# Two more operand pairs for the context's weight columns, a group of adaLN rows on TensorE, and x's squares moved up, in a one-core hybrid diffusion layer

## The chip, the cores and the metric

The kernel runs on 1 core of one Trainium2 chip. The metric is the device time of one execution in microseconds, the median of 3 runs. TensorE (PE in the profile) multiplies, VectorE (DVE) and ScalarE (ACT) work on tiles in SBUF and PSUM, GpSimd (POOL) on tiles in SBUF, and SyncE (SP) issues most of the DMAs.

## The reference, cut to what matters

One layer (DEPTH = 1) of a trunk over 2048 latent tokens of width 1024, with a context of 256 tokens in front. What the changed code computes is the beginning:

```python
ada   = silu(c) @ w_ada + b_ada            # (1, 6*1024), for the latent
ada_c = silu(c_ctx) @ w_ada + b_ada        # (6*1024,), for the context
sh1, sc1, g1, sh2, sc2, g2 = split(ada, 6);  csh1, csc1, ... = split(ada_c, 6)
hc = rmsnorm(ctx, norm_mix) * (1 + csc1) + csh1
logf_f, k_f, logf_b, k_b, vc = hgrn2_gates(hc @ w_in[:, :3 * 512])   # context: gates and values only
h  = rmsnorm(x, norm_mix) * (1 + sc1) + sh1
o  = token_mixers(h @ w_in, start states of the context)             # two gated scans, a gMLP
```

Behind that come the output projection, a gated MLP with a 3x3 convolution, and a final norm. All is float32, and a product that counts is made of three: each operand is split into a high part (rounded to TensorE's fp32r) and a low part (the rest), and hi·hi, hi·lo and lo·hi are summed in PSUM.

## The kernel before, in words

The edited code is the first 100 us. There is a part under `tc.manual_schedule()`, in which every engine takes its instructions in the order in which they are written; what follows is ordered by the framework's scheduler, with `pin` keeping single instructions in place, and with two task queues (`hg_q`, `bg_q`) whose steps are due by a count of TensorE work (`T.t`).

**adaLN.** The first 2048 columns of `w_ada` (shift and scale) are loaded as four groups of 512 columns: groups 0 and 1 (the shift) into the tile of tag `xl`, groups 2 and 3 (the scale) into that of tag `xh`. Later `xl` and `xh` hold x's low and high parts. `ada_products(g, k0, k1)` multiplies a group on TensorE with both vectors (context and latent) at once: eight products with a 128x512 block each, into a `pj` bank; `ada_rows` copies the two rows on ACT, `ada_columns` turns them into columns with four small transposes, `put_ada` adds the bias. Groups 0, 2 and 3 go that way. Group 1 goes by `ada_sums(w, k0, k1)`: for `w` = 1 (context) and `w` = 0 (latent), DVE adds eight scaled blocks into `acc` (L290), and `ada_ones` sums over partitions with four small products with `ones`.

**Context columns.** Each of the 12 context blocks (`keys` (column, CTX)) takes 128 columns of `w_in`: for head 0 the columns at 0, HW and 2·HW (first, second and third column below), for head 1 three more, and so on. `load_raw` loads a column to one of three `raw` tiles, `split_w` splits it: ACT casts the high part `whi` (L131), DVE or POOL subtracts for the low part `wlo` (L132; `w_n` counts the splits and picks the engine). There are two pairs of `whi`/`wlo` tiles, numbered in `w_free`; a pair is free again when the block's last product is done. A context block is 24 products of 128x256 (8 values of k, three each); its gate sigmoids (L547, L548, into `cS` for head 0 and `cf` for head 1) or its copy to `vv` follow on ACT. `ctx_mod(k)` makes the context's operands `ch`/`cl`. The first block's products for k = 0 to 3 are opened by hand (`opened`), and `run_banks` does the rest.

**x.** `x_start` takes x's first four rows of tiles (`xg`): ACT squares them (L232), POOL makes the root, DVE scales all four (L238), TensorE transposes them, and `x_mod` modulates (L243, `xfl`) and splits into `xh`/`xl`. Then the same with the next four (`xk`). Meanwhile `ctx_state` runs the context's scan on DVE in levels (L501 on `cS` or `cf`, L508 on `tot`). `misc` loads the masks and casts them on DVE (L461).

Of the kernel before, what the change touches and what calls it, by code (L numbers as in the profile page):

```python
# [10 lines left out]
F32R = mybir.dt.float32r  # L11
# [7 lines left out]
P = 128  # L19
D = 1024  # L20
NK = D // P
SEQ = 2048
TH = SEQ // 2
# [60 lines left out]
def tile_trunk(ctx, tc, x, c, cx, c_ctx, w_ada, b_ada, norm_mix, norm_ffn, w_in, hg_norm, sgu_g, sgu_b,  # L84
# [44 lines left out]
    def split(hi, lo, raw, eng=None, keep=lambda i: i):  # L129

        keep(S.copy(hi, raw))  # L131
        (eng or G).tensor_sub(lo, raw, hi.bitcast(F32))  # L132

    def mm3(ps, lhi, llo, rhi, rlo, first, last):
        T.matmul(ps, lhi, rhi, start=first, stop=False)
        T.matmul(ps, lhi, rlo, start=False, stop=False)
        T.matmul(ps, llo, rhi, start=False, stop=last)


    class Pump:  # L140
# [3 lines left out]
        def __init__(self):  # L144
            self.tasks, self.soon, self.at = [], [], 0.0
# [43 lines left out]
    with es1:  # L189
# [16 lines left out]
        def raw_tile():  # L206
            return p1.tile([P, D], F32, tag="raw", name="raw", bufs=3)

        w_n, w_raw, w_free = [0], {}, [0, 1]

        def load_raw(key):
            raw = raw_tile().rearrange("p (k c) -> p k c", c=P)
# [3 lines left out]
        def split_w(key, eng=None):  # L216
            if key not in w_raw:
                load_raw(key)
            raw, at = w_raw.pop(key), w_free.pop(0)
            hi = p1.tile([P, NK, P], F32R, tag=f"whi{at}", name="whi", align_bytes=AL)  # L220
            lo = p1.tile([P, NK, P], F32R, tag=f"wlo{at}", name="wlo", align_bytes=AL)
            w_n[0] += 1
            split(hi, lo, raw, eng or (V if w_n[0] < 8 or w_n[0] < 20 and w_n[0] % 2 else G))
            return hi, lo, at

        def x_sums():
            return pm.tile([P, 8], F32, tag="xss", name="xss", bufs=2)
# [50 lines left out]
        def ada_rows(g, tag):  # L278
            rows[g] = pm.tile([2, 512], F32, tag=tag, name="rows", bufs=2)
            S.copy(rows[g], pa.pop(g)[:2, :])  # L280
# [7 lines left out]
        def ada_sums(w, k0, k1):  # L288
            for k in range(k0, k1):
                V.scalar_tensor_tensor(out=acc[:, w, :], in0=wts[1, k // 4][:, k % 4, :], scalar=cs2[:, k, w:w + 1],  # L290
                                       in1=acc[:, w, :], op0=ALU.mult, op1=ALU.add)

        def ada_ones(w, to, o):
            for j in range(4):
                T.matmul(to[:, o + 2 * j:o + 2 * j + 2], acc[:, w, j * P:(j + 1) * P], ones[:, :2], start=True, stop=True)
            put_ada(1, to[:, o:o + 8].rearrange("p (j u) -> p u j", u=2)[:, :1, :], w, w + 1)
# [26 lines left out]
        def ctx_products(c, ks):  # L323
            hi, lo, _ = nxt[c, CTX]
            pj = opened[c, CTX]
            for k in ks:
                mm3(pj[:, :CTX], hi[:, k, :], lo[:, k, :], chl[:, k, :], cll[:, k, :], k == 0, False)

        xg = [ph.tile([P, D], F32, tag=t, name="xg", bufs=2) for t in ("vt", "vt", "sgt", "sgt")]
        x_rows = [x[i * P:(i + 1) * P, :] for i in range(2 * NCH)]  # L330
# [1 line left out]
        with tc.manual_schedule():  # L332
            load_ada(2)
            for i in range(2):
                ld(xc[i], cx[0][i * P:(i + 1) * P, :])
            vr = pm.tile([66, P], F32, tag="gu", name="vr", bufs=2)
            for a, n, r0 in ((norm_mix[0], 8, 0), (b_ada[0, 0:2 * D], 16, 50), (norm_ffn[0], 8, 8), (hg_norm[0], 4, 16),
                             (sgu_g[0], 4, 20), (sgu_b[0], 4, 24), (conv_b[0], 22, 28)):
                S.dma_start(vr[r0:r0 + n, :], a.rearrange("(r p) -> r p", p=P))
            load_ada(0)  # L340
            load_raw((0, CTX))
            load_ada(1)
            load_ada(3)
# [24 lines left out]
            load_raw((2 * HW, CTX))  # L368
            for i in range(4):
                ld(xg[i], x_rows[i])  # L370
            ada_products(3, 0, 1)
            ada_columns(0)
            ada_products(3, 1, 8)
            ctx_mod(0)
            ada_sums(1, 5, 8)
            for k in range(1, 4):
                ctx_mod(k)
                ada_sums(0, k - 1, k)
            nxt[HW, CTX] = split_w((HW, CTX), V)
            ss0 = x_sums()  # L380
            x_square(xg[:1], ss0, keep=lambda i: i)
            ada_rows(3, "ot")
            ada_ones(1, small, 256)
            ada_columns(3)
            opened[0, CTX] = bank("pj")
            ctx_products(0, range(4))
            for k in range(4, NK):
                ctx_mod(k)
            ada_sums(0, 3, 8)
            ada_ones(0, small, 288)  # L390
        xl = p1.tile([P, NK, TH], F32R, tag="xl", name="xl", align_bytes=AL)
        xh = p1.tile([P, NK, TH], F32R, tag="xh", name="xh", align_bytes=AL)

        def x_first(g0, xs):
            for k in range(NK):
# [10 lines left out]
        def x_start():  # L406
            xk = [pk.tile([P, 2, D], F32, tag="K", name="xk", bufs=2, align_bytes=AL) for i in range(2)]
            xs = [xk[i // 2][:, i % 2, :] for i in range(4)]
            ss, ss2 = ss0, x_sums()
            for q in range(2):  # L410
                x_square(xg[2 * q + 1:2 * q + 3], ss, 2 * q + 1)
                for i in range(2 * q, 2 * q + 2):
                    pin(ld(xs[i], x_rows[4 + i]))
                if q:
                    x_scale(xg, ss)
                yield 2.0
            for i, w in enumerate(x_first(0, xg)):
                if i in (1, 2):
                    x_square(xs[2 * i - 2:2 * i], ss2, 2 * i - 2)
                if i == 3:  # L420
                    x_scale(xs, ss2)
                yield w
            done.add("x0a")
            yield 3.0
            yield from x_first(4, xs)
# [29 lines left out]

        def misc():

            for l in range(0, 8, 4):
                mf = pm.tile([P, 4, P], F32, tag="gu", name="mf", bufs=2)
                ld(mf, masks.rearrange("p (l j) -> p l j", j=P)[:, l:l + 4, :])  # L460
                V.tensor_copy(msk[:, l:l + 4, :], mf)  # L461
            yield 1.0
            wsr = pm.tile([P, NH, P], F32, tag="nt", name="wsr", bufs=2)
            ld(wsr, w_sp[0].rearrange("h p q -> p h q"))
            bsb = pm.tile([P, NH, P], F32, tag="nt", name="bsb", bufs=2)
            ld(bsb, b_sp[0:1].broadcast_to([P, NH, P]))
            yield 5.0
            pv = bank("mi")
            for h in range(NH):
                T.transpose(pv[:, h * P:(h + 1) * P], wsr[:, h, :], ident)  # L470
            V.tensor_copy(wsT, pv.rearrange("p (h q) -> p h q", q=P))
            yield 2.5
            pv = bank("mi")
# [38 lines left out]
        def run_banks(banks, peek=None):  # L512
# [3 lines left out]
            for i, (col, n0, n, sink, pre) in enumerate(banks):  # L516
                if pre is not None:
                    pre()
                up = list(dict.fromkeys(keys[i:] + tail))
                for key in up[:2]:  # L520
                    if key not in nxt:
                        nxt[key] = split_w(key)
                if len(up) > 2 and up[2] not in w_raw and up[2] not in nxt and any(k[1] == CTX for k in up[:3]):
                    load_raw(up[2])
                hi, lo, at = nxt[keys[i]]
                hiT, loT = (chl, cll) if n == CTX else (xh, xl)
                pj = opened.pop(keys[i], None)
                k0 = 0 if pj is None else 4
                pj = pj or bank("pj")
                sl = slice(n0, n0 + n)  # L530
                for k in range(k0, NK):
# [5 lines left out]
                sink()(n0, n, pj[:, :n])  # L537
                slot()
                if keys[i] not in keys[i + 1:]:
                    w_free.append(nxt.pop(keys[i])[2])  # L540

        def tile_banks(col, sink, W=TH, pre=None):
            return [(col, n0, min(512, W), sink, pre if n0 == 0 else None) for n0 in range(0, W, 512)]
# [1262 lines left out]
```

## Time and profile before

| | |
|---|---|
| median of 3 runs | 2478.01 us (2476.81 to 2480.18) |
| the profiled execution | 2477.96 us, its span 2476.2 us |
| PE busy | 2421.4 us (98%) |
| DVE busy | 1784.7 us (72%) |
| ACT, POOL busy | 968.2 us (39%), 1053.7 us (43%) |
| mean granted TensorE clock | 0.996 |

Times in the profile count from the span's start, and matmuls are pipelined, so that a busy PE is not PE at its peak. The rows of a timeline have start, length, engine, line, operation, output<-inputs, shapes, the number of instructions merged in the row, and in brackets the engine's idle time before it and what ended it. An instruction's length includes some latency; the next may start about 0.1 us before its end.

### The profile page before, as it was taken

The numbers are of one execution on the slowest core, as the hardware profiler recorded it, in microseconds if no ns is written. First come the engines' busy times: TensorE is split into PE (matmuls) and PEld (weight loads), VectorE is DVE, ScalarE is ACT, GpSimd is POOL, SyncE is SP. The second block draws the span as 40 slices with busy tenths as digits, with TensorE's granted clock in tenths as the row PEclk, the third lists the DMA queues.
The fourth block names the chain that finished last, engine by engine and source line by source line (L and its number), as shares of the span: only waits on it lengthen the run. The fifth ranks groups of instructions, "written<-read, shape, count | busy, mean of one in ns | idle before, by whom it ended". The sixth has DMA issues, their size and how long they took to land.

```text
span 2476.2 us, 32805 instructions
## 1 busy us (share of the span) xinstructions
PE 2421.4 (98%) x11859; PEld 2009.7 (81%) x11859; DVE 1784.7 (72%) x2374; ACT 968.2 (39%) x1614; POOL 1053.7 (43%) x866
## 2 busy tenths in 40 slices
PE   7899999999999999999999999999999999999998
PEld 4787888788888888788878888888878888888887
DVE  5766875645765866465699778759999993776876
ACT  3454334434344443244443333334333342432343
POOL 1344232332333433100588787887878770000002
PEclk9999999999999999999999999999999999999999
DMA  8365445573353422768932222472222239834645
GB/s 304 96 191 184 128 137 189 177 261 120 103 182 129 144 99 86 241 210 258 310 106 90 89 80 90 143 273 86 83 93 85 91 101 354 309 120 153 225 149 195
DMA packets 307854, 400.12 MB, mean 162 GB/s; under 512 B 33113, under 2 KB 216161, under 8 KB 304621
## 3 DMA queue, kind: packets, MB, share of 16 engines
q1 hardware_dynamic: 304404, 397.28, 48.3%
q8 instruction: 94, 1.54, 0.3%
q10 hardware_dynamic: 3289, 0.76, 0.1%
q14 instruction: 67, 0.55, 0.1%
HBM read 288.85 MB, written 109.13 MB: 161 GB/s over the span
## 4 chain that ended last, share of the span: by engine, by line
PE 37%; DVE 7%; issue 3%; POOL 2%; ACT 1%; DMA 1%; SPq 0%; POOLq 0%; ACTq 0%; DVEq 0%
PE up L65 23%; PE dn L65 14%; DVE dn L1373 3%; DVE edges L1378 1%; DVE gp L1454 1%; ACT dn L1370 1%; POOL Al L132 0%; DMA yd<-fl 0%; POOL ra L1665 0%; POOL rr L1666 0%; DVE keep L1448 0%; POOL raw L1191 0%; DVE keep L1464 0%; ACT Ah L131 0%; ACT cv L1392 0%
## 5 line engine op out<-in xcount | busy, mean ns | idle before, releaser
L1373 DVE SCALAR_TENSOR_TENSOR dn<-gp,taps,dn 128x1024 f32<-128x1024 f32 x352 | 448.6, 1281 | 21.1 <-ACT dn L1370 17.9
L65 PE MATMUL up<-yf,Ah 128*128 128x512 f32 x1232 | 393.5, 389 | 0.0
L65 PE MATMUL dn<-thl,mhl 128*128 128x512 f32 x1680 | 381.5, 389 | 1.2 <-ACT thl L131 1.2
L132 POOL TENSOR_TENSOR Al<-raw,Ah 128x512 fp32r<-128x512 f32 x264 | 343.0, 1308 | 89.5 <-ACT Ah L131 81.4
L65 PEld LDWEIGHTS dn<-thl,mhl 128*128 128x128 f32 x1680 | 315.0, 188 | 67.7 <-ACT thl L131 2.0
L65 PE MATMUL pj<-xh,whi 128*128 128x512 f32 x896 | 363.8, 406 | 0.0
L65 PE MATMUL pj<-xh,wlo 128*128 128x512 f32 x896 | 350.8, 392 | 1.2 <-DVE wlo L132 1.2
L65 PE MATMUL pj<-xl,whi 128*128 128x512 f32 x896 | 350.3, 391 | 1.2 <-POOL xl L132 1.0
L65 PE MATMUL up<-xah,Al 128*128 128x512 f32 x704 | 275.5, 391 | 3.4 <-POOL Al L132 3.1
L65 PE MATMUL up<-xah,Ah 128*128 128x512 f32 x704 | 274.6, 390 | 0.6 <-ACT Ah L131 0.6
L65 PEld LDWEIGHTS up<-yf,Ah 128*128 128x128 f32 x1232 | 231.2, 188 | 47.9
L131 ACT CAST Ah<-raw 128x512 fp32r<-128x512 f32 x264 | 160.6, 618 | 276.3 <-PE up L65 213.7
L132 POOL TENSOR_TENSOR wlo<-raw,whi 128x1024 fp32r<-128x1024 f32 x55 | 135.5, 2464 | 250.3 <-ACT whi L131 224.3
L65 PE MATMUL up<-xal,Ah 128*128 128x512 f32 x528 | 205.5, 389 | 0.0
L65 PE MATMUL up<-yf,Al 128*128 128x512 f32 x528 | 205.2, 389 | 0.0
L65 PEld LDWEIGHTS pj<-xh,wlo 128*128 128x128 f32 x896 | 168.3, 188 | 37.5 <-DVE wlo L132 1.7
L65 PEld LDWEIGHTS pj<-xh,whi 128*128 128x128 f32 x896 | 168.8, 188 | 32.8 <-issue 3.5
L65 PEld LDWEIGHTS pj<-xl,whi 128*128 128x128 f32 x896 | 168.9, 189 | 31.8 <-POOL xl L132 1.8
L65 PE MATMUL dn<-wo,o 128*128 128x512 f32 x768 | 182.9, 394 | 1.8 <-DVE nt L706 0.9
L65 PEld LDWEIGHTS dn<-wo,o 128*128 128x128 f32 x768 | 141.9, 188 | 31.7 <-issue 1.1
L65 PEld LDWEIGHTS up<-xah,Al 128*128 128x128 f32 x704 | 132.1, 188 | 36.0 <-POOL Al L132 8.6
L1665 POOL TENSOR_SCALAR ra<-ss 128x1 f32<-128x1 f32 x8 | 5.3, 662 | 359.8 <-ACT jk L1657 359.8
(317 smaller groups left out, 4186.9 us busy)
## 6 DMA issues: line engine op xcount, KB each, us to landing
raw<-in_w_up_dram SPq DMA_DIRECT2D x88, 512.0 KB, 4.5
mr<-m SPq DMA_DIRECT2D x85, 512.0 KB, 5.3
raw<-in_w_in_dram SPq DMA_DIRECT2D x68, 512.0 KB, 4.3
sT<-wd SPq DMA_DIRECT2D x88, 256.0 KB, 4.4
raw<-in_w_ada_dram SPq DMA_DIRECT2D x32, 512.0 KB, 3.9
yf<-yd SPq DMA_DIRECT2D x14, 1024.0 KB
m<-cv SPq DMA_DIRECT2D x22, 544.0 KB, 2.7
raw<-in_w_down_dram SPq DMA_DIRECT2D x22, 512.0 KB, 3.8
```

What stands on the lines that cost most here:

```text
L65: return self.engine.matmul(out, lhsT, rhs, **kw)
L131: keep(S.copy(hi, raw))
L132: (eng or G).tensor_sub(lo, raw, hi.bitcast(F32))
L1370: S.activation(cr, gt[:, 0:RH, 0:GW], AF.Identity, bias=cvb[:, f:f + 1], scale=taps[:, f:f + 1])
L1373: V.scalar_tensor_tensor(out=cr, in0=gt[:, t // 3:t // 3 + RH, t % 3:t % 3 + GW], scalar=taps[:, t * NF + f:t * NF + f + 1], in1=cr, op0=A ...
L1378: V.scalar_tensor_tensor(out=e[:, 0, :], in0=gt[:, 1, t % 3:t % 3 + GW], scalar=taps[:, t * NF + f:t * NF + f + 1], in1=e[:, 0, :], op0=AL ...
L1454: V.tensor_add(g_rows(hh, f + c, n2), quad(p, kind), quad(add, kind))
L1665: G.tensor_scalar(out=a, in0=ss, scalar1=plus, scalar2=None, op0=ALU.add)
```

## The change

1. `w_free` has four pairs. The pairs 2 and 3 lie in the upper half of `xh` (columns 512 to 1023 of each k), which x's second four rows of tiles fill later; they are used once each, by the third and fourth column, and not given back. The class `Rows` reads them as [k] blocks of 128 columns. For this `xh` is allocated inside the manual part, and the third column is split there, on DVE. Up to four columns are split ahead as long as `w_n` is at most 3.
2. Group 1 for the latent is no longer summed on DVE. `ada_products(1, ...)` does two products after each `ctx_mod(k)` for k = 4 to 7, with the first context block's three products of that k in between; `ada_rows` copies the rows, and `ada_latent` transposes them and takes the latent's column alone. The context's half of group 1 stays with `ada_sums(1, ...)`.
3. x's first four squares stand in the manual part: the second one ahead of the last `ctx_mod`s, the third and fourth behind the third column's split.
4. The eighth split's low part is made by DVE instead of POOL (`w_n[0] < 9`), and the masks' casts are pinned behind `misc`'s first pause.

```diff
-        w_n, w_raw, w_free = [0], {}, [0, 1]
+        w_n, w_raw, w_free = [0], {}, [0, 1, 2, 3]
...
-            hi = p1.tile([P, NK, P], F32R, tag=f"whi{at}", name="whi", align_bytes=AL)
-            lo = p1.tile([P, NK, P], F32R, tag=f"wlo{at}", name="wlo", align_bytes=AL)
             w_n[0] += 1
-            split(hi, lo, raw, eng or (V if w_n[0] < 8 or w_n[0] < 20 and w_n[0] % 2 else G))
-            return hi, lo, at
+            if at < 2:
+                hi = p1.tile([P, NK, P], F32R, tag=f"whi{at}", name="whi", align_bytes=AL)
+                lo = p1.tile([P, NK, P], F32R, tag=f"wlo{at}", name="wlo", align_bytes=AL)
+                split(hi, lo, raw, eng or (V if w_n[0] < 9 or w_n[0] < 20 and w_n[0] % 2 else G))
+                return hi, lo, at
+            hi, lo = (xh[:, k:k + 2, 512:] for k in (4 * at - 8, 4 * at - 6))
+            split(hi, lo, raw.rearrange("p (a b) c -> p a (b c)", a=2), eng or V, pin if at > 2 else lambda i: i)
+            return Rows(hi), Rows(lo), at
...
+        def ada_latent():
+            o = 288
+            for j in range(4):
+                T.transpose(small[:, o + 2 * j:o + 2 * j + 2], rows[1][:, j * P:(j + 1) * P], ident[:2, :2])
+            put_ada(1, small[:, o:o + 8].rearrange("p (j w) -> p w j", w=2)[:, :1, :], 0, 1)
...
             for k in range(1, 4):
                 ctx_mod(k)
-                ada_sums(0, k - 1, k)
             nxt[HW, CTX] = split_w((HW, CTX), V)
             ss0 = x_sums()
             x_square(xg[:1], ss0, keep=lambda i: i)
             ada_rows(3, "ot")
+            x_square(xg[1:2], ss0, 1, keep=lambda i: i)
             ada_ones(1, small, 256)
             ada_columns(3)
             opened[0, CTX] = bank("pj")
             ctx_products(0, range(4))
             for k in range(4, NK):
                 ctx_mod(k)
-            ada_sums(0, 3, 8)
-            ada_ones(0, small, 288)
+                ada_products(1, 2 * k - 8, 2 * k - 6)
+                ctx_products(0, (k,))
+            ada_rows(1, "ot")
+            ada_latent()
+            xh = p1.tile([P, NK, TH], F32R, tag="xh", name="xh", align_bytes=AL)
+            nxt[2 * HW, CTX] = split_w((2 * HW, CTX), V)
+            x_square(xg[2:3], ss0, 2, keep=lambda i: i)
+            x_square(xg[3:4], ss0, 3, keep=lambda i: i)
         xl = p1.tile([P, NK, TH], F32R, tag="xl", name="xl", align_bytes=AL)
-        xh = p1.tile([P, NK, TH], F32R, tag="xh", name="xh", align_bytes=AL)
...
-                V.tensor_copy(msk[:, l:l + 4, :], mf)
+                mfs.append(mf)
             yield 1.0
+            for l in range(2):
+                pin(V.tensor_copy(msk[:, 4 * l:4 * l + 4, :], mfs[l]))
...
-                for key in up[:2]:
-                    if key not in nxt:
+                for key in up[:2 if w_n[0] > 3 else 4]:
+                    if key not in nxt and w_free:
                         nxt[key] = split_w(key)
...
-                k0 = 0 if pj is None else 4
+                k0 = 0 if pj is None else NK
```

How the instructions stand, at three places. On ACT, from the third column's cast on, before: (`raw_255` is the third column, `raw_405` the fourth, `pj_317` the first block's bank, `xg_156` to `xg_159` x's rows)

```order
L131 CAST whi_401<-raw_255 128x1024
L547 ACTIVATE cS_359<-pj_317 128x256
L548 ACTIVATE cS_359<-pj_317 128x256
L232 ACTIVATE xjk_395,xss_301<-xg_157 128x1024
L547 ACTIVATE cS_359<-pj_407 128x256
L232 ACTIVATE xjk_397,xss_301<-xg_158 128x1024
L548 ACTIVATE cS_359<-pj_407 128x256
L232 ACTIVATE xjk_434,xss_301<-xg_159 128x1024
L131 CAST whi_446<-raw_405 128x1024
```

And now, from x's second square on (`raw_401` is the fourth column, `pj_333` group 1's bank, `pj_316` the first block's):

```order
L246 ACTIVATE xjk_303,xss_298<-xg_157 128x1024
L337 ACTIVATE ch_154<-mi_147,s1_72,a1_71 128x256 x2
L337 ACTIVATE ch_154<-sc_148,s1_72,a1_71 128x256 x2
L294 COPY rows_366<-pj_333 2x512
L131 CAST xh_373<-raw_255 128x2x512
L246 ACTIVATE xjk_376,xss_298<-xg_158 128x1024
L575 ACTIVATE cS_382<-pj_316 128x256
L246 ACTIVATE xjk_378,xss_298<-xg_159 128x1024
L131 CAST xh_373<-raw_401 128x2x512
```

The second square moved ahead of the `ctx_mod`s (L337), the copy of group 1's rows came in ahead of the third column's cast, and the last square is followed at once by the fourth column's cast.

On DVE, from the last `ctx_mod` to x's first scaling, before:

```order
L319 TENSOR_TENSOR cl_155<-xfl_342,ch_154 128x256
L290 SCALAR_TENSOR_TENSOR acc_151<-wa_124,cs2_75,acc_151 128x512 x2
L132 TENSOR_TENSOR wlo_402<-raw_255,whi_401 128x1024
L290 SCALAR_TENSOR_TENSOR acc_151<-wa_124,cs2_75,acc_151 128x512 x3
L501 TENSOR_TENSOR cS_359<-cS_359 128x128x2
L508 TENSOR_TENSOR tot_535<-cS_359 128x256
L301 TENSOR_TENSOR s1_72<-sc_196,bc_153 128x4
L501 TENSOR_TENSOR cS_359<-cS_359,tot_535 128x64x2x2
L238 TENSOR_SCALAR xg_156<-xg_156,rs2_440 128x1024
```

And now:

```order
L339 TENSOR_TENSOR cl_155<-xfl_357,ch_154 128x256
L321 TENSOR_TENSOR s1_72<-sc_196,bc_153 128x4
L132 TENSOR_TENSOR xh_373<-raw_255,xh_373 128x2x512
L132 TENSOR_TENSOR xh_373<-raw_401,xh_373 128x2x512
L252 TENSOR_SCALAR xg_156<-xg_156,rs2_412 128x1024
```

The five sums are gone, the scan's first steps on `cS` moved behind the scaling, and the fourth column's low part moved ahead of it.

On DVE again, ahead of the scaling of the next x rows (`xk`), before:

```order
L132 TENSOR_TENSOR wlo_633<-raw_581,whi_632 128x1024
L243 TENSOR_SCALAR xfl_670<-mi_665,a1_71,s1_72 128x512
L132 TENSOR_TENSOR xl_357<-xfl_624,xh_358 128x512
L501 TENSOR_TENSOR cf_360<-cf_360 128x128x2
L243 TENSOR_SCALAR xfl_679<-mi_674,a1_71,s1_72 128x512
L461 CAST msk_128<-mf_869 128x512
L461 CAST msk_128<-mf_872 128x512
L132 TENSOR_TENSOR xl_357<-xfl_679,xh_358 128x512
L238 TENSOR_SCALAR xk_392<-xk_392,rs2_685 128x1024 x2
L238 TENSOR_SCALAR xk_393<-xk_393,rs2_685 128x1024 x2
```

And now:

```order
L132 TENSOR_TENSOR wlo_632<-raw_580,whi_631 128x1024
L132 TENSOR_TENSOR xl_381<-xfl_623,xh_373 128x512
L257 TENSOR_SCALAR xfl_669<-mi_664,a1_71,s1_72 128x512
L257 TENSOR_SCALAR xfl_678<-mi_673,a1_71,s1_72 128x512
L132 TENSOR_TENSOR wlo_693<-raw_635,whi_692 128x1024
L132 TENSOR_TENSOR xl_381<-xfl_678,xh_373 128x512
L252 TENSOR_SCALAR xk_407<-xk_407,rs2_684 128x1024 x2
L252 TENSOR_SCALAR xk_408<-xk_408,rs2_684 128x1024 x2
L527 TENSOR_TENSOR cf_383<-cf_383 128x128x2
```

The masks' casts left, `cf`'s first step moved behind the scaling, and the eighth column's low part (`wlo_693`, on POOL before) came in. From the scan's third level on `cf` and the transposes at about 100 us on, all engines have the same order as before.

More of the change, by code (lines that the diff above doesn't have):

```diff
@@ L207, in raw_tile, with __init__, __getitem__ @@
             return p1.tile([P, D], F32, tag="raw", name="raw", bufs=3)
-        w_n, w_raw, w_free = [0], {}, [0, 1]
+        class Rows:
+            def __init__(self, ap):
+                self.ap = ap
+            def __getitem__(self, at):
+                k = at[1]
+                return self.ap[:, k // 4, (k % 4) * P:(k % 4) * P + P]
+        w_n, w_raw, w_free = [0], {}, [0, 1, 2, 3]
         def load_raw(key):
@@ L326, in ctx_products @@
             for k in ks:
-                mm3(pj[:, :CTX], hi[:, k, :], lo[:, k, :], chl[:, k, :], cll[:, k, :], k == 0, False)
+                mm3(pj[:, :CTX], hi[:, k, :], lo[:, k, :], chl[:, k, :], cll[:, k, :], k == 0, k == NK - 1)
         xg = [ph.tile([P, D], F32, tag=t, name="xg", bufs=2) for t in ("vt", "vt", "sgt", "sgt")]
@@ L409, in x_start @@
             ss, ss2 = ss0, x_sums()
[L410 to L416, printed above, removed]
+            x_scale(xg, ss)
+            for i in range(4):
+                pin(ld(xs[i], x_rows[4 + i]))
+                if i % 2:
+                    yield 2.0
             for i, w in enumerate(x_first(0, xg)):
@@ L456, in misc @@
         def misc():
+            mfs = []
             for l in range(0, 8, 4):
@@ L539, in run_banks @@
                 if keys[i] not in keys[i + 1:]:
-                    w_free.append(nxt.pop(keys[i])[2])
+                    at = nxt.pop(keys[i])[2]
+                    if at < 2:
+                        w_free.append(at)
         def tile_banks(col, sink, W=TH, pre=None):
```

## The prediction

> **What bounds the kernel now.** First the page: TensorE (PE) is busy for nearly the whole span. Then the stretches of the first 140 us, where the edited code runs. In each row stand the length, then PE, PEld, DVE, ACT and POOL busy, the granted clock, the DMA share and GB/s.
>
> ```profile
> PE 2421.4 (98%) x11859; PEld 2009.7 (81%) x11859; DVE 1784.7 (72%) x2374; ACT 968.2 (39%) x1614; POOL 1053.7 (43%) x866
> ...
> 45.00:50.00 5.00, 3.46 (x25) 2.93 (x24) 4.75 (x8) 4.00 (x9) 0.00 (x0) 1.00 0.31 91
> 50.00:55.00 5.00, 3.60 (x26) 2.83 (x24) 4.07 (x9) 3.48 (x6) 1.22 (x2) 1.00 0.94 299
> 55.00:60.00 5.00, 4.75 (x28) 4.48 (x29) 5.00 (x7) 1.41 (x3) 1.69 (x1) 0.66 0.36 105
> 60.00:70.00 10.00, 9.46 (x78) 8.89 (x76) 8.82 (x18) 8.60 (x16) 4.02 (x4) 1.00 0.37 107
> 70.00:80.00 10.00, 7.22 (x35) 5.73 (x35) 9.89 (x12) 4.23 (x9) 6.09 (x4) 0.94 0.37 105
> 80.00:90.00 10.00, 9.36 (x64) 8.59 (x62) 7.30 (x13) 4.79 (x10) 2.57 (x2) 0.88 0.01 2
> 90.00:100.00 10.00, 7.59 (x34) 5.12 (x35) 9.54 (x18) 3.45 (x6) 3.08 (x2) 1.00 0.32 112
> 100.00:120.00 20.00, 20.00 (x115) 17.45 (x114) 11.63 (x26) 8.68 (x16) 5.97 (x4) 1.00 0.37 110
> ```
>
> Between 45 and 100 us PE is busy 45.4 of 55 us and DVE 49.4: here DVE sets the pace. From 100 us PE has no idle time. What PE's waits of the first 200 us say (total, times, longest) agrees: behind the start's wait for loads, the longest end on DVE instructions.
>
> ```profile
> PE mi L69 <- DVE xfl L243: 2.9, 3, 1.1
> PE mi L69 <- DVE xk L238: 2.6, 3, 1.9
> ```
>
> The order of both kernels is the same on every engine, row for row, from the place that before reaches at about 100 us. So the change is worth the lead that PE has there, and no more: a PE without a gap carries that lead on. At most it is the 9.6 us of idle time, and some 3 us lost to a clock under 1.00 in three of the rows, less what PE gets to do in addition. What it really is, DVE's chain decides.
>
> **The change part by part.** *Group 1's sums.* Eight DVE instructions of 0.75 us (6.0 us) go; the other eight, for the context's own group, stay. Instead PE runs eight products and four small transposes, and four small products with `ones` go.
>
> ```profile
> L290 DVE SCALAR_TENSOR_TENSOR acc<-wa,cs,acc 128x512 f32<-128x512 f32 x16 | 12.0, 750 | 0.5 <-DMA wa<-in_w_ada_dram 0.2
> ...
> L65 PE MATMUL pj<-wa,cs 128*2 128x512 f32 x48 | 26.1, 698 | 9.7 <-DMA wa<-in_w_ada_dram 9.7
> ...
> 12.62 7.05 PE L65 MATMUL pj<-wa,cs 128*2 128x512 f32 x16
> 39.83 0.38 PE L69 MATMUL sc<-ident,rows 2*128 2x2 f32 x4 [0.35 <-DVE s L301]
> 50.73 0.95 PE L65 MATMUL sc<-ones,acc 128*128 128x2 f32 x8
> ```
>
> A product costs 7.05/16 = 0.44 us in a run at full clock, 0.70 at worst (the mean of one, latency and slow stretches included). I take 0.44, since PE is at full clock there: 8 x 0.44 + 0.38 - 0.95 = 3.0 us more on PE. Up to 100 us PE's idle time covers them; without that cover they would cost 3.0 us.
>
> *The third and fourth pair and x's squares.* Before, ACT cast the third column at 46.00, as soon as the first column's pair was free. Now the cast needs no free pair, but it stands behind the copy of group 1's rows, and that waits for the last product.
>
> ```profile
> 40.59 0.28 PE L65 MATMUL pj<-ch,whi 128*128 128x256 f32 x1
> 40.71 0.28 PE L65 MATMUL pj<-cl,whi 128*128 128x256 f32 x1
> ...
> 38.54 0.57 ACT L280 COPY rows<-pj 2x512 f32<-2x512 f32 x1 [0.96 <-PE pj L65]
> 46.00 1.04 ACT L131 CAST whi<-raw 128x1024 fp32r<-128x1024 f32 x1 [1.51 <-PE pj L65]
> 46.95 0.38 ACT L547 ACTIVATE cS<-pj 128x256 f32<-128x256 f32 x1
> 47.49 1.06 ACT L232 ACTIVATE xjk<-xg 128x1024 bf16<-128x1024 f32 x1
> 48.44 0.20 ACT L232 ACTIVATION_READ_ACCUMULATOR xjk<-xg 128x1 f32 x1
> ...
> 47.07 1.23 DVE L132 TENSOR_TENSOR wlo<-raw,whi 128x1024 fp32r<-128x1024 f32 x1
> 52.76 2.74 DVE L238 TENSOR_SCALAR xg<-xg,rs 128x1024 f32<-128x1024 f32 x4 [0.55 <-POOL rs L126]
> ```
>
> PE starts the context products at 40.2 (39.83 + 0.38). Twelve of them at 0.12 (the step from 40.59 to 40.71), eight ada products, and nine context products in between give 40.2 + 1.4 + 3.5 + 1.1 = 46.2; 0.26 (0.70 - 0.44) is the last product's latency, so the copy starts at 46.5. Behind it ACT runs copy, cast, square, sigmoid, square, cast: 0.57 + 1.04 + 1.26 + 0.38 + 1.26 + 1.04 = 5.5, to 52.0. Then DVE's low part of the fourth column, 1.23, in front of x's scaling: 53.1 (a tenth off for the overlap of ACT's rows), against 52.76. So x is not scaled sooner: two squares have moved up, but the last one moved behind the two casts. POOL's root is ready earlier and doesn't decide. With 0.70 for a product all this is 2.1 us later.
>
> On SP's queue the fourth column's load now goes ahead of the loads of the next four x rows, which land later by that one load of 512 KB. They are first read at 63.75, with no wait in front, so this costs nothing; without that cover it would be one load's time.
>
> ```profile
> 63.75 1.05 ACT L232 ACTIVATE xjk<-xk 128x1024 bf16<-128x1024 f32 x1
> ```
>
> *From x's scaling to the next x rows' scaling.* This is one DVE chain, 52.76 to 77.17 before, 24.4 us long, and busy but for 1.2 us (a wait for POOL that stays).
>
> ```profile
> 50.45 0.63 DVE L501 TENSOR_TENSOR cS<-cS 128x256 f32<-128x256 f32 x1
> 50.92 0.42 DVE L508 TENSOR_TENSOR tot<-cS 128x256 f32<-128x256 f32 x1
> 51.79 0.42 DVE L501 TENSOR_TENSOR cS<-cS,tot 128x256 f32<-128x256 f32 x1
> ...
> 61.19 0.81 DVE L243 TENSOR_SCALAR xfl<-mi,a,s 128x512 f32<-128x512 f32 x1 [1.18 <-POOL xl L132]
> ...
> 71.45 2.16 DVE L132 TENSOR_TENSOR xl<-xfl,xh 128x512 fp32r<-128x512 f32 x1
> 73.53 1.73 DVE L501 TENSOR_TENSOR cf<-cf 128x256 f32<-128x256 f32 x1
> 75.79 0.75 DVE L461 CAST msk<-mf 128x512 uint8<-128x512 f32 x2
> 76.56 0.69 DVE L132 TENSOR_TENSOR xl<-xfl,xh 128x512 fp32r<-128x512 f32 x1
> 77.17 2.73 DVE L238 TENSOR_SCALAR xk<-xk,rs 128x1024 f32<-128x1024 f32 x4
> 81.32 1.66 DVE L243 TENSOR_SCALAR xfl<-mi,a,s 128x512 f32<-128x512 f32 x2 [1.42 <-PE mi L69]
> ...
> 69.68 3.38 POOL L132 TENSOR_TENSOR wlo<-raw,whi 128x1024 fp32r<-128x1024 f32 x1
> ```
>
> In: cS's first steps, which stood ahead of the scaling (0.47 + 0.42 + 0.42 by their starts and lengths: +1.3). Out: the mask's casts (-0.75) and cf's first step (-0.63, its length where nothing disturbs it, as for cS). As many low parts as before stand in the chain, four; the fourth is the eighth column's, which before ran on POOL, and the one for the fourth column moved ahead of it. With POOL's 3.38 gone I let the xl that ran beside it shrink from 2.16 to 0.69 (-1.5). The sum is -1.6: the second scaling starts at 53.1 + 22.8 = 75.9, 1.2 us sooner than at 77.17. If the collision only moves to another instruction, -0.1 and no gain; if cf's (1.73 for 0.63) goes too, 1.1 more.
>
> The Trainium skill, GPSIMD Engine Reference, 1. Specifications, has GpSimd share its SBUF interfaces with VectorE, with contention for DVE instructions with two SBUF inputs. By that rule each POOL low part left collides with whatever two-input instruction DVE has then, and the lead here would be 0; the rows show such collisions, but only beside some POOL instructions.
>
> *Behind the second scaling* DVE waited 1.42 for PE, which ran its transposes slowly. cf's first step now fills 0.63 of it. If PE needs as long again the lead stays 1.2; at full clock it becomes 2.0. I take 1.5. The mask's casts now stand where DVE has room (11.6 busy of 20 from 100 us).
>
> The profiled execution took 2477.96 us (span 2476.2), the median of the runs is 2478.01. So: 2477.96 - 1.5 = 2476.5 us. With products at 0.70 the lead is -0.6, with the collision moved 0.0, with both collisions gone 2.6 to 3.1. With 1 us more for the clock's phase on either side this case's own range is 2474 to 2480. A measurement of this kernel can tell about 0.2% (5 us) from no change, so the forecast is: within it.
>
> **The rivals.** *Most of the stage's waits and collisions go.* Six us less on DVE, PE's third and fourth column without a wait, no slow clock at 55 us: then PE sets the pace, and the lead is what PE had idle or slow, 9.6 + 3, less 3.0 and less the waits that must remain (for POOL 1.2, for x's second scaling 1.9): 6.5, 2471.5 us, 2468.5 to 2473. For it: DVE does have less to do at 45 us. Against it: these six us lay ahead of the scaling, and the scaling waits for ACT. Chance 0.28.
>
> *The clock falls where it didn't.* PE now has its early work done sooner, and meets the sixth column's low part, which DVE delivers no sooner than before:
>
> ```profile
> 64.33 1.21 DVE L132 TENSOR_TENSOR wlo<-raw,whi 128x1024 fp32r<-128x1024 f32 x1
> 65.60 0.39 PE L65 MATMUL pj<-ch,wlo 128*128 128x256 f32 x1 [0.49 <-DVE wlo L132]
> ...
> 78.06 0.30 PE L69 MATMUL mi<-ident,xk 128*128 128x128 f32 x1 [1.92 <-DVE xk L238]
> ```
>
> PE's work ahead of it is 122 context products (14.6), the 3.5, and some 3 of transposes: about 62 us with changes between kinds, so it idles 2 to 3 us instead of 0.49. After 1.92 idle at 78.06 the clock was 0.88 in the next ten us. If that happens at 65, the column's remaining 22 products take 2 us more, ACT's next casts and POOL's root come as much later, and the second scaling is at 77.9 rather than 75.9: 0.7 late, 2478.7. It becomes slower by over 5 us only if PE's later waits halve the clock two or three times more: 2483 to 2485. It decides once PE idles about 2 us there. Chance 0.20, 0.12 of it slower by over 0.2%.
>
> The Trainium skill, TensorE: Matmul & The Clock Gate, Why this matters for your kernels, wants gaps of over about 3 us before the clock drops. The trace differs, with 1.92 before 0.88. By the page this rival would not occur, and the lead would be the 2.0 of full clock, 2476.0 us.
>
> *The extra pairs do nothing:* three `raw` buffers and ACT's order hold the columns as before, and nothing moves at PE's 100 us: 2478.0. Chance 0.05.
>
> **How the numbers follow.** The forecast has 0.47, the extra pairs 0.05, and the clock within the bound 0.08: together 0.60 within 0.2%. Faster 0.28, slower 0.12. The range leaves out the lower part of the first rival (under 2470, about 0.1) and the slow end (over 2482, about 0.1).
>
> **What would show it.** Right: the first scaling of x at about 53, PE without a wait from 46 to 57, the second scaling at about 76, PE's first wait at 62 to 65, and a lead of 1 to 2 us at 100 us that stays. Wrong: a first scaling before 51 or after 55, no wait of PE at 62 to 65, a clock of 0.5 there, or a lead at 100 us that isn't the lead at the end.

## The result, and the profile after

The changed kernel takes 2483.51 us (median of 21 runs, 2479.38 to 2488.75), the kernel before, in the same comparison, 2477.68 (21 runs, 2473.81 to 2481.26). The ratio is 1.0022, 95% interval 1.0016 to 1.0029: slower by 4.0 to 7.2 us, where 2476.5 (2470 to 2482) was predicted.

First the same stretches as in the prediction, of the changed kernel (length; PE, PEld, DVE, ACT, POOL busy; granted clock, DMA share, GB/s).

```profile
45.00:50.00 5.00, 5.00 (x22) 1.96 (x20) 0.00 (x0) 1.18 (x2) 0.00 (x0) 1.00 0.71 221
50.00:55.00 5.00, 5.00 (x43) 5.00 (x43) 2.72 (x4) 5.00 (x11) 1.22 (x2) 1.00 0.36 93
55.00:60.00 5.00, 5.00 (x45) 5.00 (x44) 5.00 (x7) 2.40 (x6) 0.00 (x0) 1.00 0.56 176
60.00:70.00 10.00, 7.52 (x56) 6.87 (x55) 8.68 (x18) 6.36 (x14) 2.63 (x2) 0.94 0.28 82
```

PE now has no gap from 45 to 60 us, and DVE, which was busy 4.75 of the first 5 us, does nothing at all there. The timeline shows what it stands behind. PE first (start, length, engine, line, operation):

```profile
37.89 0.38 PE L69 MATMUL sc<-ident,rows 2*128 2x2 f32 x4 [0.35 <-DVE s L321]
39.83 1.88 PE L65 MATMUL pj<-wa,cs 128*2 128x512 f32 x4
...
46.91 1.88 PE L65 MATMUL pj<-wa,cs 128*2 128x512 f32 x4
49.62 0.40 PE L69 MATMUL sc<-ident,rows 2*128 2x2 f32 x4
```

Then ACT and DVE; in brackets stand the idle time ahead of an instruction and what ended it.

```profile
48.82 0.58 ACT L294 COPY rows<-pj 2x512 f32<-2x512 f32 x1 [6.27 <-PE pj L65]
49.30 1.04 ACT L131 CAST xh<-raw 128x1024 fp32r<-128x1024 f32 x1
52.60 1.03 ACT L131 CAST xh<-raw 128x1024 fp32r<-128x1024 f32 x1
...
50.06 0.16 DVE L321 TENSOR_TENSOR s<-sc,bc 128x4 f32<-128x4 f32 x1 [6.48 <-PE sc L69]
50.37 1.23 DVE L132 TENSOR_TENSOR xh<-raw,xh 128x1024 fp32r<-128x1024 f32 x1
53.67 1.23 DVE L132 TENSOR_TENSOR xh<-raw,xh 128x1024 fp32r<-128x1024 f32 x1 [2.07 <-ACT xh L131]
54.81 2.73 DVE L252 TENSOR_SCALAR xg<-xg,rs 128x1024 f32<-128x1024 f32 x4
```

Of `wa` there are four such rows (the first and the last are shown), each of four instructions and two of the eight products (two after each `ctx_mod`): a float32 product is two PE instructions here, and takes 1.88/2 = 0.94 us. ACT waits 6.27 us for the last of them with the copy of group 1's rows; the third column's cast, two squares and the fourth column's cast stand behind that copy. DVE is idle for 6.48 us: the next instruction in its order, `s`, needs PE's transposes of the copied rows, and the third column's low part stands behind it. x's first scaling begins at 54.81 instead of 52.76. What follows downstream, one row of PE and two of DVE:

```profile
67.65 0.39 PE L65 MATMUL pj<-ch,wlo 128*128 128x256 f32 x1 [2.21 <-DVE wlo L132]
...
66.38 1.21 DVE L132 TENSOR_TENSOR wlo<-raw,whi 128x1024 fp32r<-128x1024 f32 x1
79.38 2.74 DVE L252 TENSOR_SCALAR xk<-xk,rs 128x1024 f32<-128x1024 f32 x4 [1.18 <-POOL rs L126]
```

PE waits 2.21 us for the sixth column's low part, where it waited 0.49, and the second scaling is at 79.38 instead of 77.17.

Two profiles do not begin alike. Group 3's products ran at a lower clock in before's profile, and all that follows began later there. So times of two profiles are counted here from PE's four transposes of group 3's rows (39.83 before, 37.89 after), and not from the span's start.

```profile
30.00:35.00 5.00, 5.00 (x10) 1.01 (x10) 3.55 (x7) 3.13 (x7) 0.00 (x0) 0.55 1.10 351
...
30.00:35.00 5.00, 5.00 (x11) 0.93 (x10) 3.30 (x7) 3.62 (x9) 0.00 (x0) 0.87 1.10 358
```

The first row is before's (clock 0.55), the second the changed kernel's (0.87). Counted so, x's first scaling is 4.0 us late (54.81 - 37.89 = 16.92 against 52.76 - 39.83 = 12.93), and the second 4.2. At 100 us, at a wait of PE that both kernels have, it is 3.2 us (61.76 against 58.57):

```profile
98.40 0.50 PE L65 MATMUL pj<-xh,wlo 128*128 128x512 f32 x1 [0.26 <-DVE wlo L132]
...
99.65 0.50 PE L65 MATMUL pj<-xh,wlo 128*128 128x512 f32 x1 [0.26 <-DVE wlo L132]
```

At the spans' ends it is 5.6 us (2479.9 - 37.89 against 2476.2 - 39.83), close to the 5.8 us between the medians. So about 2.4 us of this pair of profiles are lost behind 100 us. That the change loses them there isn't shown: counted in the same way, the twelve other profiles of the experiments drift by -1.4 to +4.3 us against before's between 100 us and the end, though their instructions stand in the same order there.

### The profile page after: what moved, and what is told of

The parts are those of the page before. It is cut to its first block, busy times and chain, and to the rows that moved or that the text cites. A ratio compares the mean times of both kernels' runs of the same rounds, so it can differ in the third digit from the quotient of the medians.

```text
span 2479.9 us, 32819 instructions
## 1 busy us (share of the span) xinstructions
PE 2426.5 (98%) x11871; PEld 2008.2 (81%) x11871; DVE 1779.3 (72%) x2367; ACT 968.3 (39%) x1615; POOL 1049.7 (42%) x865
## 4 chain that ended last, share of the span: by engine, by line
PE 41%; DVE 10%; issue 4%; POOL 2%; ACT 2%; DMA 1%; SPq 0%; POOLq 0%; ACTq 0%; DVEq 0%
PE up L65 21%; PE dn L65 19%; DVE dn L1401 5%; DVE edges L1406 2%; DVE gp L1482 1%; ACT dn L1398 1%; PE up L69 0%; POOL Al L132 0%; PE pj L65 0%; POOL ra L1693 0%; DVE keep L1476 0%; DMA raw<-in_w_up_dram 0%; DMA raw<-in_x_dram 0%; POOL rr L1694 0%; DVE keep L1492 0%
```

## The experiments

Three theories stood at first. **A, the held copy:** ACT's copy of group 1's rows waits for the eight products, and holds the third cast and all behind it. **B, PE's work:** the products are 7.5 us that PE's idle time doesn't cover. **C, the pairs:** their place in `xh`, or the later order of the splits, costs the time. Each timed kernel is compared with runs of the kernel before on the same chip; a wide interval of 0.9991 to 1.0008 is about -2 to +2 us.

**sums_back** keeps all of the change except that the latent's group 1 is summed on DVE again (the last three sums behind the third column's split and x's squares), and **cast_first** keeps the products on PE and moves the copy behind the third column's split and two squares:

```diff
 # cast_first
-            ada_rows(1, "ot")
-            ada_latent()
             xh = p1.tile([P, NK, TH], F32R, tag="xh", name="xh", align_bytes=AL)
             nxt[2 * HW, CTX] = split_w((2 * HW, CTX), V)
             x_square(xg[2:3], ss0, 2, keep=lambda i: i)
             x_square(xg[3:4], ss0, 3, keep=lambda i: i)
+            ada_rows(1, "ot")
+            ada_latent()
```

Expected of sums_back:

> The changed kernel, but with group 1's latent half summed on DVE again (eight sums, four small products with ones); pairs, squares, eighth split and masks stay changed. Theory A (the held copy: eight products of 0.94 us, 1.88 for two, hold ACT's copy of group 1's rows to 48.8, and with it the third column's cast, two squares and x's first scaling): the copy is gone, x's first scaling at about 51 to 53, and the time 2476 to 2478, as before or up to 2 us less. Theory B (the products cost PE 7.5 us that nothing covers, whoever waits for them): the same, 2476 to 2478. Theory C (the pairs in xh or the later order of the splits cost the time): still 2481 to 2484.

Expected of cast_first:

> The changed kernel with the third column's cast and x's third and fourth square written ahead of the copy of group 1's rows, the eight products stay on PE. Theory A: ACT no longer waits 6.3 us; the third column's cast at about 43, x's first scaling at 47 to 49 (6 us sooner than 54.8), PE's wait of 2.2 us for the sixth column's low part gone, and the time 2477 to 2479. Theory B: PE's work is the same, so the time stays at 2482 to 2484. Theory C: 2481 to 2484.

Measured: sums_back 2477.17 us, ratio 0.9997 (0.9988 to 1.0006); cast_first 2478.02, ratio 1.0000 (0.9991 to 1.0008). The loss is gone in both. The rows of cast_first, ACT and DVE:

```profile
40.74 1.03 ACT L131 CAST xh<-raw 128x1024 fp32r<-128x1024 f32 x1
47.08 0.58 ACT L294 COPY rows<-pj 2x512 f32<-2x512 f32 x1 [3.07 <-PE pj L65]
...
41.81 1.23 DVE L132 TENSOR_TENSOR xh<-raw,xh 128x1024 fp32r<-128x1024 f32 x1
49.78 2.74 DVE L252 TENSOR_SCALAR xg<-xg,rs 128x1024 f32<-128x1024 f32 x4
```

PE runs the same eight products, and the copy still waits for them; but the third cast has gone before it, and x's first scaling stands at 49.78: counted from the transposes (36.12) at 13.7, where the changed kernel has 16.9 and before 12.9. The same work on PE and none of the loss: B falls, A is shown. DVE still waits 5.29 us for the transposes of group 1's rows in this kernel, and the scaling misses the expected 47 to 49; what no longer waits is the third column's split and two squares.

**half_products** leaves out four of the latent's eight products (one after each `ctx_mod`), so half of that sum is missing.

> The changed kernel with four of the latent's eight products (the other four are left out, so half of that sum is missing). Theory A, the held copy: by the rows of the changed kernel two products take 1.88 us, so four fewer free the copy of group 1's rows 3.8 us sooner, and the third column's low part, x's first scaling and the end follow: 2483.5 - 3.8 = 2479.7 us (2478.5 to 2481.0). Rival D, a threshold: the delay of the third cast decides by whether x's blocks then collide with the sixth column's low part, not by its size; then half the delay gives nothing or everything: within 0.7 us of 2483.5 or of 2477.7.

Measured: 2478.72, ratio 1.0004 (0.9995 to 1.0013), some 4.5 us sooner than the changed kernel (1.0022 - 1.0004), for four products of 0.94 (3.8 us). The copy comes at 45.52, x's first scaling at 51.52 (15.2 from the transposes, which stand at 36.37 there; one of the products ran at half clock in this profile). By the medians that is in proportion or slightly more: theory A's own figure, 2479.7, lies 1 us above the median and inside the interval. Rival D's second branch, nothing or everything, isn't excluded (2477.7 is as near).

```profile
45.52 0.58 ACT L294 COPY rows<-pj 2x512 f32<-2x512 f32 x1 [4.42 <-PE pj L65]
51.52 2.74 DVE L252 TENSOR_SCALAR xg<-xg,rs 128x1024 f32<-128x1024 f32 x4
```

**early_group** was a try to gain: the whole of group 1, for the latent and the context, on PE while it waits for group 3's load, and no sums on DVE.

> The changed kernel with all of group 1 (both vectors) on PE ahead of group 3, where PE waited 2.5 us for group 3's load and then ran at half the clock; no DVE sums, no products with ones, no copy behind the context's modulation. Theory A and B: 8 x 0.9 = 7.0 us of products, of which 2.5 fill the wait and some 3 come back from the clock; the context starts at 38 to 40 as before, the third cast at 43 to 44, x's first scaling at 47 to 49, and the time 2472 to 2476. Theory C: 2479 or more.

Measured: 2478.93, ratio 1.0003 (0.9994 to 1.0012), a miss. Seven us of products took the place of a 2.5 us wait, and PE's transposes of group 3's rows came at 41.64. x's first scaling, counted from there, was early (51.77, so 10.1 against 12.9), and the start had lost what that gained.

**no_pairs** takes the two pairs away and leaves the rest of the change; **pairs_alone** is the kernel before with the two pairs and nothing else.

```diff
 # no_pairs, on the changed kernel
-        w_n, w_raw, w_free = [0], {}, [0, 1, 2, 3]
+        w_n, w_raw, w_free = [0], {}, [0, 1]
 ...
-            nxt[2 * HW, CTX] = split_w((2 * HW, CTX), V)
 ...
-                for key in up[:2 if w_n[0] > 3 else 4]:
+                for key in up[:2]:
```

Expected of no_pairs:

> The changed kernel with two operand pairs only, as before, and the third column split by the scheduled part; products, squares, eighth split and masks stay changed. Theory A: the copy still stands ahead of the third cast, the fourth and fifth columns wait for a pair besides: 2483 to 2486. Theory B: 2483 to 2484. Theory C: 2477 to 2480.

Expected of pairs_alone:

> The kernel before with only the two further operand pairs (no products moved, squares as before). From no_pairs against the changed kernel the pairs are worth about 1 us: 2476.7 us (2476.0 to 2477.3). Rival: where the cast of the third column comes early anyway, the pairs are not waited for, and the time is that of before: 2477.7. Under theory A neither is near the changed kernel's 2483.5.

Measured: no_pairs 2484.47, ratio 1.0027 (1.0016 to 1.0037): the pairs aren't what costs, C falls. pairs_alone 2474.64, ratio 0.9988 (0.9979 to 0.9997): **faster than both kernels**, by 3.0 us against before (0.7 to 5.2), and by its median more than either theory expected, though the 1 us of the first lies inside the interval. Its rows (ACT, DVE, then a stretch):

```profile
41.45 1.04 ACT L131 CAST xh<-raw 128x1024 fp32r<-128x1024 f32 x1
...
50.07 0.16 DVE L315 TENSOR_TENSOR s<-sc,bc 128x4 f32<-128x4 f32 x1 [0.27 <-PE sc L65]
51.94 2.74 DVE L252 TENSOR_SCALAR xg<-xg,rs 128x1024 f32<-128x1024 f32 x4 [0.71 <-POOL rs L126]
57.64 1.22 DVE L132 TENSOR_TENSOR wlo<-raw,whi 128x1024 fp32r<-128x1024 f32 x1
...
45.00:50.00 5.00, 5.00 (x44) 5.00 (x44) 4.41 (x7) 4.14 (x10) 0.00 (x0) 1.00 1.16 301
```

The third column is cast at 41.45, not at 46.00; PE does context columns without a gap to 50 us beside DVE's sums; and the sixth column's low part is done by DVE at 57.64, where before had it at 64.33 and the changed kernel, where PE waited 2.21 us for it, at 66.38. Counted from the transposes (38.02) the cast is at 3.4 instead of 6.2, and the low part at 19.6 instead of 24.5 and 28.5; x's first scaling is no sooner (13.9 against 12.9). So what comes sooner is the columns, not x.

The pairs bring 3 us by themselves, sums_back (the pairs with all else but the products) less than 1. The two intervals overlap, so by themselves they don't show that something takes the rest; the other runs ask. **cast_both** is cast_first with the fourth column's split ahead of the copy too, **sums_both** the same split ahead of sums_back's last three sums.

> cast_first, and the fourth column's cast and low part too ahead of the copy of group 1's rows. In cast_first's profile DVE waits 5.29 us for PE's transposes of group 1's rows with the fourth low part and x's scaling (49.78) behind it. If DVE sets the pace there, x's scaling starts once its constants are there, about 46 us, and the end comes up to 3 us sooner: 2475 us (2474 to 2476.5). If TensorE sets it, which is busy 5.00 us of every 5 from 45 to 65 us in cast_first, nothing is gained: 2478.0 (2477.3 to 2478.8).

> sums_back, and the fourth column's cast and low part by hand ahead of the last three sums. In sums_back x's scaling starts at 49.41 and the last sums' constant at 50.64 is what the second scaling waits for. If x's start sets the pace: 2476.5 us (2475.5 to 2477.2). If not, as sums_back: 2477.2.

Measured: cast_both 2477.13, ratio 0.9998 (0.9989 to 1.0007); sums_both 2477.17, ratio 0.9999 (0.9990 to 1.0008). No gain over the kernels they come from that these runs can tell: an earlier fourth column isn't shown to be what is missing. (cast_both's median lies between its two expectations.) In cast_both x's first scaling stands behind the constants from PE all the same (50.56, `s` at 50.47).

**pairs_squares, pairs_nine, pairs_masks, pairs_products** add one part of the change each to pairs_alone: x's squares and scaling sooner, the eighth low part on DVE, the masks' casts later, the products with the copy in their old place.

> pairs_alone, and x's squares sooner with x's scaling as in the changed kernel (the second square behind group 3's rows, the third and fourth at the end of the part written by hand). sums_back, which has all of the change but the products, was 2477.2 us; pairs_alone 2474.6. Theory E, x too soon: with the squares done sooner x's blocks go ahead of the sixth column's low part on DVE, PE waits 2.2 us for it (62.52 in sums_back) and its clock falls: 2477.2 (2476.3 to 2478.2). Rival F, an earlier start of x is worth something: 2473.5 (2472.5 to 2474.3).

> pairs_alone, and the eighth column's low part on DVE instead of POOL. It takes 1.21 us on DVE, which is busy nearly all of 55 to 95 us, and takes 2.39 us from POOL, which there meets DVE's transfers (cf 2.09 and xl 1.72 beside it). If DVE's count decides: 1.2 us later, 2475.8. If the meeting costs as much: 2474.6 (2474.0 to 2475.2). Theory E expects nothing of it: 2474.6.

> pairs_alone, and the masks' two conversions on DVE (0.41 us each) put at the later place that the changed kernel gives them. They move from 72.6 to about 95 us: 0.8 us off DVE before x's second scaling, back before the columns that follow. Theory E and rival F expect 2474.6 (2474.0 to 2475.2); if the masks are what takes the rest of pairs_alone's gain back, 2477.

> pairs_alone, and the latent's group 1 on TensorE as in the changed kernel; the squares stay late. Theory A: the copy of group 1's rows again waits for 7.5 us of products with the third column's cast behind it, so that column's low part comes about 4 us later than in pairs_alone's rows, and x's squares, which stand behind it too, push x's first scaling to 55 us or later: 2482 to 2485 us. If the products only hurt together with the squares sooner: 2474.6 to 2476.

Measured, with the time of x's two scalings in the profile (from the span's start) and that of the transposes of group 3's rows:

| kernel | transposes | first | second | median us | ratio to before (95%) |
|---|---|---|---|---|---|
| before | 39.83 | 52.76 | 77.17 | 2477.68 | 1 |
| pairs_alone | 38.02 | 51.94 | 75.01 | 2474.64 | 0.9988 (0.9979 to 0.9997) |
| pairs_nine | 37.27 | 52.58 | 75.46 | 2475.57 | 0.9992 (0.9983 to 1.0000) |
| pairs_masks | 37.27 | 51.19 | 73.67 | 2476.25 | 0.9993 (0.9985 to 1.0002) |
| pairs_squares | 38.48 | 48.09 | 76.38 | 2479.64 | 1.0004 (0.9995 to 1.0013) |
| pairs_products | 37.17 | 55.75 | 79.34 | 2480.90 | 1.0016 (1.0007 to 1.0024) |
| after | 37.89 | 54.81 | 79.38 | 2483.51 | 1.0022 (1.0016 to 1.0029) |
| no_pairs | 38.56 | 53.93 | 83.45 | 2484.47 | 1.0027 (1.0016 to 1.0037) |

The three kernels of this table with a copy that holds x's squares on ACT have the three longest times, and the second scaling 41.5 to 44.9 us behind the transposes; the other five have it at 36.4 to 38.2. pairs_products shows the hold with the squares late: its third cast, against what was expected, had gone ahead (40.88), but all three squares stand behind the copy. Its time falls short of the 2482 to 2485 that theory A gave; that the products hurt only together with the earlier squares (2474.6 to 2476) falls.

```profile
48.13 0.58 ACT L294 COPY rows<-pj 2x512 f32<-2x512 f32 x1 [5.66 <-PE pj L65]
49.23 1.06 ACT L246 ACTIVATE xjk<-xg 128x1024 bf16<-128x1024 f32 x1
...
55.75 2.74 DVE L252 TENSOR_SCALAR xg<-xg,rs 128x1024 f32<-128x1024 f32 x4 [1.19 <-POOL rs L126]
```

pairs_squares gives pairs_alone's gain back, and more than theory E's number. In its profile x's scaling starts at 48.09, 4.3 us sooner counted from the transposes, and DVE's four scalings stand between the last sums:

```profile
48.09 0.75 DVE L252 TENSOR_SCALAR xg<-xg,rs 128x1024 f32<-128x1024 f32 x1 [1.26 <-POOL rs L126]
48.76 0.75 DVE L304 SCALAR_TENSOR_TENSOR acc<-wa,cs,acc 128x512 f32<-128x512 f32 x1
...
54.62 0.16 DVE L315 TENSOR_TENSOR s<-sc,bc 128x4 f32<-128x4 f32 x1 [0.42 <-PE sc L65]
62.20 1.21 DVE L132 TENSOR_TENSOR wlo<-raw,whi 128x1024 fp32r<-128x1024 f32 x1
```

So the sums end 4.1 us later, again from the transposes (`s` at 54.62, against 50.07 in pairs_alone), x's blocks run ahead of the sixth column's low part, which comes at 62.20 instead of 57.64, and the second scaling is 0.9 later than in pairs_alone though the first was earlier. That this is what takes the gain isn't shown: the profiled execution took 2474.84 us, the shortest of its eleven and as short as pairs_alone's median. Its clock stays 1.00 from 35 us to the last few us; but the four shortest executions have a mean clock of 0.998, the seven others, from 2478.57 us on, 0.996 or 0.997. So theory E's clock isn't ruled out. The two ratios' intervals just touch, so the size (about 4 us) is uncertain. Of the eighth low part and the masks the runs tell nothing apart from pairs_alone.

## Why the prediction was wrong

**The step that failed is the price of a product.** The prediction read 7.05 us for `x16` as sixteen products of 0.44. The count of a row is one of PE instructions, and a float32 product is two: the row was eight products of 0.88. In the changed kernel they took 0.94, so the term "8 x 0.44" is 3.5 where it should have been 7.5, and "+3.0 us on PE" should have been 7.0. The total row could have told it: `x48` for the three groups of eight products that before has, `x64` for four now; and so could the row beside it, where four products with `ones` stand as `x8`. The Trainium skill (FP8 and Floating Point Precision, TensorE Precision Notes) gives true FP32 four passes through the array. The trace agrees: a context product of 256 columns takes 0.12 us, so four passes over 512 columns are an estimated 4 x 2 x 0.12 = 0.96, against 0.94 measured.

```profile
L65 PE MATMUL pj<-wa,cs 128*2 128x512 f32 x64 | 32.2, 647 | 9.2 <-DMA wa<-in_w_ada_dram 9.2
```

**The path was right, and it carried the error on.** The prediction put the copy 6.3 us behind the start of the context products (40.2 to 46.5). Measured from the end of group 3's transposes (37.89 + 0.38) it was 10.55, and 6.3 + 4.0 of missing product time is 10.3. From the copy to x's scaling it had 6.6, and 6.0 was measured. The alternative that it kept (0.70 for a product, 2.1 us later) was too small a bound as well, since it too took an instruction for a product.

**The chain behind it did not shrink, because of a wait that the sum left out.** From the first to the second scaling the sum was 22.8 us; it is 79.38 - 54.81 = 24.57, as before (24.41). DVE still meets POOL's low parts:

```profile
63.90 1.37 DVE L534 TENSOR_TENSOR tot<-tot 128x128 f32<-128x128 f32 x1
70.84 1.23 DVE L527 TENSOR_TENSOR cS<-cS,tot 128x256 f32<-128x256 f32 x1
76.62 1.58 DVE L132 TENSOR_TENSOR xl<-xfl,xh 128x512 fp32r<-128x512 f32 x1
...
63.78 1.34 POOL L132 TENSOR_TENSOR xl<-xfl,xh 128x512 fp32r<-128x512 f32 x1 [1.58 <-ACT xh L131]
70.51 1.27 POOL L132 TENSOR_TENSOR xl<-xfl,xh 128x512 fp32r<-128x512 f32 x1 [5.39 <-ACT xh L131]
76.14 1.51 POOL L132 TENSOR_TENSOR xl<-xfl,xh 128x512 fp32r<-128x512 f32 x1 [4.36 <-ACT xh L131]
```

A step of `tot` on half the elements takes 1.37, where the prediction's row of a whole one has 0.42; a `cS` step takes 1.23 for 0.42, and an `xl` 1.58 for 0.69. Each of the three stands beside one of POOL's low parts of x. The Trainium skill's rule of the shared interfaces (GPSIMD Engine Reference, 1. Specifications), by which the lead was 0 here, fits these rows. Yet in sum DVE's work did shrink, nearly as forecast. These are the two chains, before's first (length; PE, PEld, DVE, ACT, POOL busy), and POOL's roots ahead of the second scaling:

```profile
52.76:77.17 24.41, 20.59 (x133) 18.20 (x133) 23.21 (x34) 14.84 (x28) 11.80 (x7) 0.93 0.46 136
54.81:79.38 24.57, 21.02 (x140) 18.67 (x138) 21.95 (x35) 15.09 (x29) 6.95 (x6) 0.93 0.40 119
...
75.25 1.01 POOL L126 TENSOR_TENSOR rs<-rs,mhalf 128x4 f32<-128x4 f32 x1
78.34 1.01 POOL L126 TENSOR_TENSOR rs<-rs,mhalf 128x4 f32<-128x4 f32 x1
```

DVE is busy 21.95 us instead of 23.21, 1.3 less, where the sum had 1.6. What ate it is the 1.18 us that DVE now waits for POOL's root, just ahead of the scaling. Before, the root was done at 76.26, in time for 77.17; now it is done at 79.35, behind ACT's squares of x and POOL's last low part. The sum had one wait for POOL, which stays (1.18, now 1.32), and put this second one at nothing. sums_back, which has no such copy to wait for, has the same 1.18, so this wait doesn't need the held copy.

Together: at the second scaling the change is 4.2 us late where 1.2 early was predicted. Of these 5.4 us 3.7 stand at the first scaling already (4.0 late against 0.3), and 1.8 come from the chain.

**The second rival came true in kind.** PE's wait for the sixth column's low part came, later than "62 to 65" (67.65) and of the size named (2.21), with a clock of 0.88 and 0.78 in the next two stretches of 5 us. Its share of the loss was not measured by itself. sums_back has the same wait (2.21 at 62.52, with a clock of 0.80 and 0.86) and not the loss, so it isn't this wait alone that costs. The Trainium skill's threshold of about 3 us for a gap (TensorE: Matmul & The Clock Gate, Why this matters for your kernels) isn't seen in this row.

```profile
65.00:70.00 5.00, 2.79 (x17) 2.35 (x17) 5.00 (x12) 3.44 (x8) 0.12 (x1) 0.88 0.21 60
70.00:75.00 5.00, 4.87 (x26) 4.13 (x26) 5.00 (x9) 3.80 (x7) 1.27 (x1) 0.78 0.22 62
```

**The lead at 100 us is not the lead at the end,** which the prediction named as a sign of being wrong (3.2 us late, then 5.6). "From 100 us PE has no idle time" was read from a row that ends at 120 us. To the span's end before's PE is busy 2341.0 of 2376.2 us, so there are 35 us of waits in which a lead can change. Whether it did so by the change or by chance stays open, as said above.

```profile
100.00:2476.20 2376.20, 2340.96 (x11457) 1958.32 (x11455) 1717.40 (x2259) 923.87 (x1533) 1032.38 (x842) 1.00 0.48 159
```

**What was right:** PE has no wait from 46 to 57; x isn't scaled sooner, since the copy stands ahead of the casts; more than half of the difference stands at 100 us. The first rival (waits and collisions go) didn't come, though its premise, that DVE has less to do, did: DVE was idle, and waited. "The extra pairs do nothing" is not borne out: pairs_alone gains by them, if just clear of no change.

## What to carry to other kernels

Work moved from a busy engine to an idle one is paid where its result is collected: in an order written by hand, put the instruction that collects it behind everything that doesn't need it. Before a row's count is divided into work, check it against a number of operations that the code fixes. And try the parts of a change alone: here one of them gains 3 us (0.7 to 5.2), and with the products and their copy beside it the gain turns into a loss.

## What the runs showed of the hardware

A float32 product of 128 x 2 by 128 x 512 is two PE instructions, 0.47 us each. And a wait of over 2 us alone does not settle the clock. From about 11 us to the last few us of these profiles, it falls to half for 3.41 us at a time, or for twice that. In stretches of 3.41 us that end where a half clock begins, the wait of 2.21 us in sums_back lies whole in one: PE is busy 1.20 us of it, and the next stretch is at 0.50. On the same grid, taken from its one earlier half clock (28.38 to 31.79), the wait of 2.27 us in pairs_squares is cut in two: PE is busy 1.80 and 1.95 us, and the clock stays 1.00.

```profile
62.52 0.39 PE L65 MATMUL pj<-ch,wlo 128*128 128x256 f32 x1 [2.21 <-DVE wlo L132]
59.61:63.02 3.41, 1.20 (x6) 0.77 (x7) 3.41 (x8) 2.57 (x6) 0.39 (x1) 1.00 0.01 2
63.02:66.43 3.41, 3.41 (x19) 3.41 (x18) 3.41 (x8) 1.35 (x3) 1.05 (x1) 0.50 0.53 154
...
70.14 0.39 PE L65 MATMUL pj<-ch,wlo 128*128 128x256 f32 x1 [2.27 <-POOL wlo L132]
65.93:69.34 3.41, 1.80 (x14) 1.36 (x12) 3.41 (x4) 3.38 (x7) 3.02 (x2) 1.00 0.18 54
69.34:72.75 3.41, 1.95 (x9) 1.52 (x10) 3.41 (x5) 1.00 (x3) 0.75 (x1) 1.00 0.40 115
```

PE's busy time in a stretch isn't the whole rule: in half_products a half clock (38.02 to 41.43) follows a stretch with 2.66 us busy. What the whole rule is, these runs don't show.
